# SwiGLU's second projection by Strassen products over all inner columns, and modulation adds on GpSimd

## The chip, the cores and the metric

The kernel runs on 1 core of one Trainium2 chip. The metric is device time in microseconds (us) of one execution. Engines are TensorE (PE, its weight loads PEld), VectorE (DVE), ScalarE (ACT), GpSimd (POOL) and SyncE (SP), which here issues the DMAs, one after the other, in a fixed order. Before the change the time is 2586.88 us, the median of 3 runs (2584.0 to 2587.2).

## The reference

One step of a diffusion model's layer, on 1024 latent and 256 context tokens of width 1024:

```
x += 1/2 * gate1 * SwiGLU_1(adaLN_1(RMSNorm(x)))
h  = adaLN_2(RMSNorm(x)); four head groups A, B, C, D of 256 channels each from h @ w_in
x += gate2 * concat(A, B, C, D) @ w_out
x += 1/2 * gate3 * SwiGLU_2(adaLN_3(RMSNorm(x)))
SwiGLU(h) = (silu(h @ w1a) * (h @ w1b)) @ w2        inner width 2816
adaLN shift/scale/gate from SiLU(c) @ w_mod + b_mod
```

Everything is fp32. The change touches the products with w2, called the down-projections, and the sums that give adaLN's shifts, scales and gates.

## The kernel before

x lies transposed in SBUF: 8 tiles of 128 channels for each of three chunks of tokens, chunk 0 and 1 with 512 latent tokens each, chunk 2 with the 256 context tokens. Every matmul operand is split into a high part, cast by ScalarE, and a low part, subtracted by VectorE, and every product is three matmuls: whi·uh, whi·ul, wlo·uh. The order of the work in time is: norm 1, first up-projection (to 644 us of the span), first down-projection (to 959), the mixer with its four head groups and w_out (to 1700), second up-projection (to 2280), second down-projection (to the end).

An up-projection runs over 22 units, one for each block of 128 inner columns, of 25.06 us each. Its latent part is computed by seven Strassen products already: the 1024 x 256 weights of a block are quartered, their sums (rsum) formed on VectorE from the two loaded halves (raw), and the four quarters of the result put together from p_b and p_t in PSUM; px is the context's. The results, v for the first half of the latent tokens, u for the second and uc for the context, go to DRAM (ud). During the first up-projection the modulation runs as well: GpSimd multiplies a block of w_mod (wh, 256 KB by DMA) with the two conditioning vectors, ScalarE sums each product over its columns (pr, wh into part), and an addition of 2 columns puts it into modT (line 598 of the listing, on VectorE). There are 112 such blocks.

A down-projection (lines 824 to 857) takes two inner blocks at a time, 11 times. It loads two w2 blocks (raw, 512 KB) and the u blocks of them (ur, 256 KB), splits them, multiplies for each chunk c and each of 8 output tiles d the two blocks into one PSUM bank, po, and adds po times the gate into x[c][d], one scalar_tensor_tensor on VectorE. After the last block of chunk c, `done(c)` starts what needs it: in the first down-projection the norm of the chunk (`norm_chunk`: squares on ScalarE, their sums on GpSimd and VectorE, nst over the partitions on TensorE, the root rt, diagonal matrices dg on VectorE, nrs on TensorE, then nt, hh, hl on VectorE, ScalarE and GpSimd) and the copy of x to DRAM (xs); in the second the output's DMAs.

The order of all this on each engine is not that of the source. Every operation is recorded as a node first, and a planner (`Plan`, `issue`) then writes the instructions out in the order that a list schedule with assumed prices gives, nodes of earlier source (with an offset that the code can set) first where they compete. Tiles of one pool and tag are given out in the order of the nodes. Afterwards every engine runs its instructions strictly in that order, and so does SyncE with the DMAs. All operations stand under one line, L394, so that the trace is read by tile names. raw has two buffers, the split weights whi and wlo four each, and po alternates over the PSUM pools PG and PT_.

## Time and profile before

| | |
|---|---|
| median of 3 runs | 2586.88 us (2584.0 to 2587.2) |
| profiled execution, its own time | 2589.14 us |
| its span | 2587.4 us |
| mean granted TensorE clock | 0.982 of 2.4 GHz |
| TensorE busy | 2491.5 us (96%), 14100 matmuls |
| VectorE busy | 1762.7 us (68%) |
| ScalarE busy | 1011.8 us (39%) |
| GpSimd busy | 572.3 us (22%) |
| DMA | 259.42 MB, mean 100 GB/s |

The span runs from the first to the last instruction of the profiled execution; 1.7 us of its time lie around it. Busy shares are averages over stages with different limits, so they are read by stretches in the section on the rows.

### The profile page before, as it was taken

The page shows a single profiled execution, that of the slowest core. Times are in us where ns is not written, and L with a number is a line of the kernel's source. Part 1 is how long each engine was busy: PE and PEld are TensorE (multiplying, and loading weights), DVE is VectorE, ACT ScalarE, POOL GpSimd, SP SyncE. Part 2 cuts the span into 40 slices and gives each one's busy share as a digit, 9 for nine tenths or more (in the row PEclk, how much of TensorE's full clock was granted, in tenths as well). Part 3 has the DMA queues.
Part 4 walks back from the last instruction along what each step waited for, and adds up shares of the span by engine and source line. Part 5 has one row for each costly group of instructions (what it writes and reads, how often), then busy time and mean ns, then how long its engine had stood idle before and what let it go on. Part 6 is the DMA issues. An engine that isn't in the chain of part 4 may idle for free.

```text
span 2587.4 us, 37285 instructions
## 1 busy us (share of the span) xinstructions
PE 2491.5 (96%) x14100; PEld 2096.2 (81%) x14100; DVE 1762.7 (68%) x2819; ACT 1011.8 (39%) x2009; POOL 572.3 (22%) x475
## 2 busy tenths in 40 slices
PE   5899999999999999999999989979999999999999
PEld 3688888888888878888778778868888888888888
DVE  7988888876877674568656575385555555587765
ACT  6555555543212046242476685252222222232110
POOL 1578778830000031122100263130000000000000
PEclk8899999999999999999999999979999999999999
DMA  7143444435422132341301234212122221362312
GB/s 262 60 141 118 146 126 143 124 104 185 150 78 86 49 106 68 103 124 66 109 31 36 81 114 142 98 37 80 54 80 67 66 74 60 97 234 86 94 50 82
DMA packets 146676, 259.42 MB, mean 100 GB/s; under 512 B 15936, under 2 KB 61504, under 8 KB 146496
## 3 DMA queue, kind: packets, MB, share of 16 engines
q1 hardware_dynamic: 146496, 257.04, 31.0%
q8 instruction: 111, 1.82, 0.3%
q14 instruction: 69, 0.57, 0.1%
HBM read 195.11 MB, written 61.87 MB: 99 GB/s over the span
## 4 chain that ended last, share of the span: by engine, by line
PE 74%; DVE 4%; ACT 2%; DMA 1%; issue 1%; POOL 0%; SPq 0%; ACTq 0%
PE po L394 23%; PE p_t L394 12%; PE p_b L394 9%; PE px L394 6%; PE pwo L394 4%; PE fb L394 3%; PE pgd L394 3%; PE ptb L394 2%; PE pyb L394 2%; PE ps L394 2%; PE pd L394 1%; DVE x L394 1%; ACT prob L394 1%; DVE dst L394 1%; PE pgate L394 1%
## 5 line engine op out<-in xcount | busy, mean ns | idle before, releaser
L394 DVE SCALAR_TENSOR_TENSOR x<-po,modT,x 128x512 f32<-128x512 f32 (+1 forms) x528 | 345.3, 661 | 159.7 <-PE po L394 158.4
L394 PE MATMUL po<-uh,whi 128*128 128x512 f32 (+1 forms) x1056 | 377.5, 358 | 5.1 <-DVE x L394 5.1
L394 ACT CAST whi<-raw 128x1024 fp32r<-128x1024 f32 x206 | 213.7, 1048 | 424.7 <-PE px L394 142.2
L394 PE MATMUL po<-uh,wlo 128*128 128x512 f32 (+1 forms) x1056 | 375.3, 355 | 0.0
L394 PE MATMUL po<-ul,whi 128*128 128x512 f32 (+1 forms) x1056 | 373.2, 353 | 0.0
L394 DVE TENSOR_TENSOR wlo<-raw,whi 128x1024 fp32r<-128x1024 f32 x206 | 281.3, 1366 | 100.4 <-ACT whi L394 96.1
L394 PEld LDWEIGHTS po<-uh,whi 128*128 128x128 f32 x1056 | 199.7, 189 | 32.2 <-DVE x L394 5.8
L394 PEld LDWEIGHTS po<-uh,wlo 128*128 128x128 f32 x1056 | 199.3, 189 | 30.9
L394 PEld LDWEIGHTS po<-ul,whi 128*128 128x128 f32 x1056 | 199.5, 189 | 29.5
L394 PE MATMUL px<-hh,whi 128*128 128x256 f32 x704 | 200.2, 285 | 2.3 <-ACT uc L394 1.2
L394 PE MATMUL px<-hl,whi 128*128 128x256 f32 x704 | 200.0, 284 | 0.7 <-DVE hl L394 0.7
L394 PE MATMUL px<-hh,wlo 128*128 128x256 f32 x704 | 198.8, 282 | 0.0
L394 POOL TENSOR_TENSOR pr<-wh,cb 128x512 f32<-128x512 f32 x112 | 172.8, 1543 | 92.3 <-DMA wh<-in_wmodT 60.7
L394 POOL TENSOR_TENSOR wh<-wh,cb 128x512 f32<-128x512 f32 x112 | 186.6, 1666 | 8.8
L394 ACT CAST uh<-ur 128x512 fp32r<-128x512 f32 x110 | 67.3, 622 | 301.7 <-DMA ur<-ud 248.0
L394 POOL TENSOR_TENSOR sq<-sq,sq 128x512 f32<-128x512 f32 (+1 forms) x32 | 37.9, 1185 | 495.3 <-ACT sq L394 492.3
L394 PEld LDWEIGHTS px<-hh,whi 128*128 128x128 f32 x704 | 135.1, 192 | 6.8 <-ACT hh L394 1.6
L394 PEld LDWEIGHTS px<-hl,whi 128*128 128x128 f32 x704 | 134.8, 192 | 5.4 <-DVE hl L394 1.3
L394 PEld LDWEIGHTS px<-hh,wlo 128*128 128x128 f32 x704 | 134.5, 191 | 0.5
L394 ACT ACTIVATE g<-g 128x512 f32<-128x512 f32 x88 | 55.6, 632 | 177.7 <-DVE g L394 177.6
L394 ACT ACTIVATE pr<-pr 128x512 f32<-128x512 f32 x112 | 70.9, 633 | 83.4 <-POOL pr L394 71.4
L394 ACT ACTIVATE wh<-wh 128x512 f32<-128x512 f32 x112 | 70.5, 629 | 56.6 <-POOL wh L394 55.8
(511 smaller groups left out, 6113.3 us busy)
## 6 DMA issues: line engine op xcount, KB each, us to landing
raw<-in_w SPq DMA_DIRECT2D x132, 512.0 KB
wh<-in_wmodT SPq DMA_DIRECT2D x112, 256.0 KB
ur<-ud SPq DMA_DIRECT2D x88, 256.0 KB
ud<-v SPq DMA_DIRECT2D x44, 256.0 KB
ud<-u SPq DMA_DIRECT2D x44, 256.0 KB
x<-in_xT SPq DMA_DIRECT2D x32, 256.0 KB
wmt<-in_wmod SPq DMA_DIRECT2D x32, 256.0 KB
xs<-x SPq DMA_DIRECT2D x32, 256.0 KB
```

Source lines behind the costliest of these rows:

```text
L394: getattr(real, meth)(*[f(v) for v in a], **{q: f(v) for q, v in k.items()})
```

## The change

A down-projection is now nine passes one after the other, each over all inner blocks k and with four PSUM banks. Two passes are the context's: 22 blocks, 256 tokens, the left and the right half of w2's columns. Seven are Strassen products for the latent tokens: inner columns in two halves of 11 blocks, output channels in two halves, tokens in the two chunks. A pass streams its weights, two blocks of 128 x 512 at a time (512 KB), and its u blocks or a sum of them, and at its end adds the four banks into every quarter of x that the product belongs to (1, 1, 1, 4, 1, 2, 2, 3 and 1 quarters). The three sums of w2's quarters and a fourth are formed during the up-projection before it, by `weight_sums` after every second unit: two loads of 512 KB, four half additions on VectorE, three writes to DRAM (sd). The sums of u blocks (t3, t1, t2, t4) are formed on VectorE within the passes. `done` is called for a chunk's half as it is finished; the copies to xs stand ahead of the norm, the tables of the mixer are asked for at its first call, and the first matmuls of the mixer (pa_) take the chunks in the order 2, 1, 0. The modulation's 112 additions go to GpSimd.

```diff
@@ modulation
-        V.tensor_tensor(modT[:, s, f], part, modT[:, s, f] if hf else smv("bmod", 8 * s + f).to_broadcast([P, 2]),
+        G.tensor_tensor(modT[:, s, f], part, modT[:, s, f] if hf else smv("bmod", 8 * s + f).to_broadcast([P, 2]),
                         ALU.add)
@@ buffers
-    BL = 2
+    HF = NFF // 2
     RAW = 2
+    sd = dp.tile([2, 4, HF, P, 512], F32, name="sd")
@@ down
-    def down(n, gate, src, after_block=None, done=None):
...
+    def weight_sums(n, k):
+        lo, hi = slice(0, 512), slice(512, 1024)
+        ra, rb = new_raw(), new_raw()
+        rs = tg.tile([P, 1024], F32, name="rsum", tag="rsum", bufs=1)
+        dma(ra, I["w2"][n, k])
+        dma(rb, I["w2"][n, HF + k])
+        V.tensor_tensor(rs[:, lo], ra[:, hi], rb[:, hi], ALU.add)
+        V.tensor_tensor(rs[:, hi], rs[:, lo], ra[:, lo], ALU.subtract)
+        dma(sd[n, 0:2, k].rearrange("i p n -> p i n"), rs.rearrange("p (i n) -> p i n", i=2))
+        V.tensor_tensor(ra[:, lo], ra[:, hi], ra[:, lo], ALU.subtract)
+        dma(sd[n, 2, k], ra[:, lo])
+        V.tensor_tensor(rb[:, lo], rb[:, lo], rs[:, hi], ALU.subtract)
+        dma(sd[n, 3, k], rb[:, lo])
+
+    def down(n, gate, src, done):
...
+        def t4(k):
+            r = load(HF + k, lo)
+            V.tensor_tensor(r, r, k22[k], ALU.subtract)
+            return r
+        PASSES = [
+            (w2[:, :, lo], None, [(2, 0)]),
+            (w2[:, :, hi], None, [(2, 1)]),
+            (w2[second, :, lo], lambda k: load(HF + k, lo), [c11]),
+            (w2[first, :, lo], lambda k: load(k, lo), [c11, c12, c21, c22]),
+            (sd[n, 3], b22, [c12]),
+            (sd[n, 2], t3, [c21, c22]),
+            (sd[n, 0], t1, [c12, c22]),
+            (sd[n, 1], t2, [c12, c21, c22]),
+            (w2[second, :, hi], t4, [c21]),
+        ]
...
+        for i, (ws, us, outs) in enumerate(PASSES):
+            nk = NFF if us is None else HF
+            w = 256 if us is None else 512
+            ps = [(PT_ if i % 2 else PG)(name="po")[:, :w] for _ in range(4)]
+            for k in range(nk):
+                if k % 2 == 0:
+                    m = min(2, nk - k)
+                    raw = new_raw()
+                    dma(raw[:, :512 * m].rearrange("p (j n) -> p j n", j=m),
+                        ws[k:k + m].rearrange("j p n -> p j n"))
+                    wh, wl = split_w(raw, 512 * m)
...
+                for d in range(4):
+                    q = slice(512 * (k % 2) + d * P, 512 * (k % 2) + (d + 1) * P)
+                    TE.matmul(ps[d], wh[:, q], uh, start=(k == 0), stop=False)
+                    TE.matmul(ps[d], wh[:, q], ul, start=False, stop=False)
+                    TE.matmul(ps[d], wl[:, q], uh, start=False, stop=(k == nk - 1))
...
+            for d in range(4):
+                for c, h in outs:
+                    v = 1 if c == 2 else 0
+                    f = 4 * h + d
+                    V.scalar_tensor_tensor(x[c][f], ps[d], modT[:, gate, f, v:v + 1], x[c][f], ALU.mult, ALU.add)
+            for o in outs:
+                left[o] -= 1
+                if left[o] == 0:
+                    done(*o)
@@ after a unit of the up-projection
+        if nu[0] % 2:
+            plan.offset += 700
+            weight_sums(0, nu[0] // 2)
+            plan.offset -= 700
@@ done1
-        norm_chunk(1, *h2[0], c)
-        for d in range(KT):
+        for d in range(4 * half, 4 * half + 4):
             dma(xs[d][:, t0:t0 + w], x[c][d])
+            tables()
+        if (c, half) in ((2, 1), (1, 1), (0, 1)):
+            norm_chunk(1, *h2[0], c)
@@ mixer's first products
-    for c, (t0, n) in enumerate(CHUNKS):
+    for c in (2, 1, 0):
```

How the planner's order moves is seen at two places. The first is SyncE's queue at the end of the first down-projection; before, the last loads of its weights (raw from w2) are followed by the mixer's and by the copies of x to xs:

```order
L394 DMA raw_7956<-in_w2 128x1024
L394 DMA raw_7970<-in_w2 128x1024
L394 DMA raw_8170<-in_wfm 128x1024
L394 DMA raw_8184<-in_wfm 128x1024
L394 DMA raw_8384<-in_wfm 128x1024
L394 DMA xs_140<-x0_5705 128x512
L394 DMA raw_8398<-in_wfm 128x1024
L394 DMA xs_140<-x0_5746 128x512
```

The changed kernel has there the last four of eight copies of chunk 1, and behind them the last weights (raw_8491) and the first u blocks (ur, from ud) of the last product:

```order
L394 DMA xs_141<-x1_6070 128x512
L394 DMA xs_141<-x1_6084 128x512
L394 DMA xs_141<-x1_6072 128x512
L394 DMA xs_141<-x1_6086 128x512
L394 DMA raw_8491<-in_w2 128x512
L394 DMA ur_8497<-ud_139 128x512
L394 DMA ur_8495<-ud_139 128x512
L394 DMA ur_8501<-ud_139 128x512
L394 DMA ur_8505<-ud_139 128x512
```

Each copy of x waits for the last addition into its tile; the u blocks that the last product subtracts from and multiplies with leave after them. On TensorE of the changed kernel, between the last matmuls of the seventh product (po_8042) and the first of the last one (po_8242, po_8252), stand the norm's matmuls of chunk 1:

```order
L394 MATMUL po_8042<-uh_8344,whi_8322 128x512
L394 MATMUL po_8042<-ul_8347,whi_8322 128x512
L394 MATMUL po_8042<-uh_8344,wlo_8326 128x512
L394 MATMUL nst_8459<-ones_203,sq1_7870 128x1 x4
L394 MATMUL nrs_8467<-dg_800,ones_203 128x128
L394 MATMUL nrs_8467<-dg_808,ones_203 128x128
L394 MATMUL nrs_8467<-dg_7009,ones_203 128x128
L394 MATMUL nrs_8467<-dg_7013,ones_203 128x128
L394 MATMUL po_8242<-uh_8361,whi_8360 128x512
L394 MATMUL po_8252<-uh_8361,whi_8360 128x512
L394 MATMUL po_8242<-ul_8365,whi_8360 128x512
```

Before, matmuls of other output tiles stood around them. The second place is SyncE's queue in a unit of the first up-projection. Before, a unit's two weight loads stand between the modulation's loads (wh) and the unit's results (ud):

```order
L394 DMA wh_2500<-in_wmodT 128x512
L394 DMA raw_2502<-in_w1 128x1024
L394 DMA ud_139<-uc_2033 128x256
L394 DMA wh_2541<-in_wmodT 128x512
L394 DMA wh_2581<-in_wmodT 128x512
L394 DMA wh_2611<-in_wmodT 128x512
L394 DMA wh_2642<-in_wmodT 128x512
L394 DMA wh_2677<-in_wmodT 128x512
L394 DMA ud_139<-v_2243 128x512
L394 DMA raw_2687<-in_w1 128x1024
```

In the changed kernel every second unit has the loads of w2, the writes of their sums (sd) and then the next unit's weights (raw from w1):

```order
L394 DMA raw_2775<-in_w2 128x1024
L394 DMA wh_2784<-in_wmodT 128x512
L394 DMA ud_139<-u_2276 128x512
L394 DMA raw_2831<-in_w2 128x1024
L394 DMA wh_2842<-in_wmodT 128x512
L394 DMA ud_139<-uc_2353 128x256
L394 DMA wh_2875<-in_wmodT 128x512
L394 DMA sd_140<-rsum_2720 128x2x512
L394 DMA sd_140<-raw_2775 128x512
L394 DMA sd_140<-raw_2831 128x512
L394 DMA wh_2928<-in_wmodT 128x512
L394 DMA cb_2941<-in_cb 128x2x512
```

The next rows of that queue are the two loads of w1, raw_2915 and raw_2921, into the same two buffers.

## Rows read from the trace of the kernel before

**Rows 1.** Busy times by stretch: its us; PE, PEld, DVE, ACT, POOL; clock, DMA share, GB/s.

```profile
12.00:110.00 98.00, 73.48 (x462) 50.23 (x463) 86.94 (x161) 57.65 (x103) 28.86 (x20) 0.79 0.43 152
...
493.74:518.80 25.06, 25.06 (x134) 21.42 (x133) 20.71 (x22) 12.90 (x30) 21.27 (x14) 1.00 0.44 131
...
644.00:936.00 292.00, 292.00 (x1510) 249.64 (x1510) 216.06 (x322) 54.45 (x75) 6.72 (x6) 1.00 0.31 96
936.00:976.00 40.00, 33.76 (x175) 28.69 (x174) 35.69 (x58) 26.30 (x44) 21.33 (x18) 0.91 0.25 90
...
952.00:956.00 4.00, 3.75 (x18) 3.46 (x18) 4.00 (x8) 2.14 (x5) 2.44 (x3) 0.50 0.61 214
...
2280.00:2587.00 307.00, 304.02 (x1584) 260.31 (x1583) 220.73 (x331) 45.98 (x63) 0.00 (x0) 1.00 0.29 94
```

**Rows 2.** The chain of waits, its last two pieces on TensorE: start, us, what.

```profile
2277.16 2.83 PE px L394 x24
2279.99 304.05 PE po L394 x1584
```

**Rows 3.** Timeline, TensorE at the seam: start, us, what, [idle before, releaser].

```profile
948.70 0.39 PE L394 MATMUL po<-uh,whi 128*128 128x256 f32 x1 [3.19 <-DVE x L394]
...
955.12 0.41 PE L394 MATMUL po<-uh,wlo 128*128 128x256 f32 x1
...
955.33 0.41 PE L394 MATMUL po<-uh,whi 128*128 128x256 f32 x1
```

**Rows 4.** Groups of VectorE: xcount, busy us, mean ns, idle before.

```profile
L394 DVE SCALAR_TENSOR_TENSOR x<-po,modT,x 128x512 f32<-128x512 f32 x352 | 262.6, 750 | 136.0 <-PE po L394 134.7
...
L394 DVE SCALAR_TENSOR_TENSOR x<-po,modT,x 128x256 f32<-128x256 f32 x176 | 83.8, 483 | 23.7 <-PE po L394 23.7
...
L394 DVE TENSOR_TENSOR modT<-part,small 128x2 f32<-128x2 f32 x56 | 44.7, 799 | 14.5 <-ACT wh L394 14.5
...
L394 DVE TENSOR_TENSOR raw<-raw,rsum 128x512 f32<-128x512 f32 x44 | 40.9, 930 | 0.0
```

**Rows 5.** Timeline at the seam, the norm's work on VectorE and GpSimd.

```profile
938.90 1.95 DVE L394 TENSOR_SCALAR dg<-ident,rt 128x128 f32<-128x128 f32 x4
...
939.49 1.27 POOL L394 TENSOR_TENSOR sq<-sq,sq 128x512 f32<-128x512 f32 x1 [0.98 <-ACT sq L394]
...
941.43 2.06 DVE L394 SCALAR_TENSOR_TENSOR nt<-x,scl,nrs 128x512 f32<-128x512 f32 x3
...
954.55 0.74 POOL L394 TENSOR_TENSOR sq<-sq 128x256 f32<-128x256 f32 x1 [0.72 <-ACT sq L394]
```

**Rows 6.** Timeline: a u block's load issued, and the cast that waits for it.

```profile
681.86 18.35 SPq L394 DMA_DIRECT2D ur<-ud  x6
...
684.56 0.62 ACT L394 CAST uh<-ur 128x512 fp32r<-128x512 f32 x1 [6.22 <-DMA ur<-ud]
```

**Rows 7.** Timeline in the mixer: two weight loads of 512 KB and their splitting.

```profile
1247.97 1.74 SPq L394 DMA_DIRECT2D raw<-in_wc  x2
...
1251.69 1.04 ACT L394 CAST whi<-raw 128x1024 fp32r<-128x1024 f32 x1
...
1253.43 1.22 DVE L394 TENSOR_TENSOR wlo<-raw,whi 128x1024 fp32r<-128x1024 f32 x1
...
1255.00 1.06 ACT L394 CAST whi<-raw 128x1024 fp32r<-128x1024 f32 x1 [2.27 <-DMA raw<-in_wc]
```

**Rows 8.** Timeline in a unit of the first up-projection: its second weight load.

```profile
500.38 0.33 SPq L394 DMA_DIRECT2D raw<-in_w  x1
...
504.26 0.69 DVE L394 TENSOR_TENSOR rsum<-raw 128x512 f32<-128x512 f32 x1 [3.24 <-DMA raw<-in_w]
...
505.69 2.23 DVE L394 TENSOR_TENSOR wlo<-raw,whi 128x1024 fp32r<-128x1024 f32 x1
```

**Rows 9.** Waits of TensorE from 12 to 110: total us, times, longest.

```profile
PE p_t L394 <- DVE t1l L394: 3.0, 2, 2.4
```

More of the change, by code (lines that the diff above doesn't have):

```diff
@@ L944, in write_down, with done1 @@
     h2 = {}
[L946 removed]
+    def done1(c, half):
         t0, w = CHUNKS[c]
+        for d in range(4 * half, 4 * half + 4):
+            dma(xs[d][:, t0:t0 + w], x[c][d])
         if not h2:
             h2[0] = ([None] * 3, [None] * 3)
[L950 to L952 removed]
+            tables()
+        if (c, half) in ((2, 1), (1, 1), (0, 1)):
+            norm_chunk(1, *h2[0], c)
     up(0, ops1, prepare, after_unit)
     assert not mods
[L956 removed]
+    down(0, 2, None, done1)
     hh, hl = h2[0]
```

101 lines of the change are left out of this document (58 added, 43 removed).

## The prediction

> **What bounds the kernel now.** I read the busy times by stretch first [rows 1]. TensorE is busy for all 292.0 us of the first down-projection's stretch, for 304.02 of 307.00 us in the second; it stands only at the start, at the seam between the first down-projection and the mixer (33.76 of 40.00 us) and in the mixer. VectorE has slack everywhere (216.06 of 292.00 us in the first down-projection). Then the chain of waits: the second down-projection is one unbroken piece of 1584 matmuls, 304.05 us, and the up-projection before it ends in px's 24 matmuls of 256 columns in 2.83 us [rows 2]. So a matmul that goes is worth its full time, and only what makes TensorE stand is a cost. At full clock a matmul of 256 columns takes 2.83 / 24 = 0.118 us, one of 512 (304.05 - 528 x 0.118) / 1056 = 0.229; the timeline shows 0.21 for 256 columns [rows 3] in the stretch with granted clock 0.50, which is 1.2 GHz [rows 1].
>
> **What goes.** Per down-projection the latent part falls from 22 inner blocks x 8 x 2 x 3 = 1056 matmuls to 7 products x 11 x 4 x 3 = 924; the context part stays at 528. That is 132 x 0.229 = 30.2 us, for both 60.4 us. VectorE loses the additions into x at every second block: 176 of 0.75 us and 88 of 0.48 per down-projection become 64 wide ones [rows 4]; it was not the bound, so this is worth nothing by itself. The 112 modulation adds (two groups of 56, 0.8 us each, [rows 4]) leave it likewise, beside a full TensorE.
>
> **The seam gains.** Before, TensorE loses 40.00 - 33.76 = 6.2 us there, waiting for the last additions into x between norm work on VectorE (3.19 us the longest, [rows 3]), and then runs some 25 matmuls of 256 columns at 1.2 GHz, which costs 25 x (0.21 - 0.118) = 2.3 us. After the change the context and the second latent chunk are finished before the last product and the mixer's first matmuls take chunks 2, 1, 0: their 4 x 24 x 0.118 + 4 x 24 x 0.229 = 33 us cover the norm of chunk 0. I take all 8.5 us.
>
> **The last product of the first down-projection costs.** On SyncE's queue the loads of its u blocks stand behind eight writes of x1, which wait for the additions of the seventh product. That product writes into three quadrants: 12 additions, about 0.66 us apart (the spacing of three such instructions in a row, [rows 5]), of which the first starts when the first bank is done, 2 us before the product's end; they end at +6. The loads leave at +7.7 and land 2.7 us later (681.86 to 684.56, [rows 6]); then subtract, cast and low part, 0.69 + 0.62 + 0.69 (the steps of 512 columns in [rows 6, 8]): +12.5 at the soonest. But TensorE's order also puts the norm's nst and nrs matmuls of chunk 1 ahead of the product. They wait for ScalarE's squares, GpSimd's sums (1.27 each, [rows 5]), the root and four dg (1.95): about +14.3, and the first ul stands behind the dg on VectorE: +15.5. Then 2.3 us for the low clock (as at the seam) and 2.2 us more for the second or third block, whose subtraction and ul stand behind a dozen norm instructions. In all 20 us; at least 11 (the loads alone with a quicker queue), at most 28 if the norm is served whole before the second block. In the second down-projection there is no norm and these loads are prepared two products earlier: 0.
>
> **The context products cost.** They come first, with 256 columns: one 512 KB load of weights serves only 24 x 0.118 = 2.83 us of TensorE. There are two load buffers, and each is held from the issue over landing, cast and low part. The mixer shows that round: issues at 1247.97 and a little over a microsecond later, casts at 1251.69 and 1255.00 (the second waited for its DMA), 1.05 for the cast, 1.22 for the low part [rows 7]. That is 3.7 to 5.6 + 1.05 + 1.22 = 6.0 to 7.9 us a buffer, 3.0 to 3.9 us a load of two: 0.2 to 1.1 us late each, against a lead of some four loads prepared during the up-projection (11 us, used once). For 22 loads that is between 22 x 0.17 - 11, which is below 0, and 22 x 1.1 - 11 = 13; the seam between the two products adds 1.9 (one addition of 0.48 and one low part of 1.22 at its end). Taken: 3.6 + 1.9 = 5.5 us per down-projection, 11 for both, a little above the middle of the two ends, since the slow one of the two loads shared its time with other transfers, as these do with the u blocks; 0 to 15 each.
>
> **The fourth pass costs** 1 us each, 2 together: its 16 additions take 16 x 0.66 = 10.6 to 16 x 0.75 = 12 us, and the four u blocks prepared ahead give 4 x 12 x 0.229 = 11.
>
> **The weight sums cost** in the up-projections. In every second unit two more 512 KB loads, four half sums and three writes go through the same two load buffers, ahead of the next unit's own weights. Before, in the unit from 493.74 the second load is issued at 500.38, summed from 504.26 and its low part done by 508 [rows 8]; the next unit starts at 518.80, so some 11 us are spare. The extra round takes a landing of 3.9 [rows 8], four sums of up to 0.93 [rows 4] and a write that has to land before the buffer is loaded again (2.7 for the nearest row, [rows 6]): 3.9 + 3.7 + 2.7 = 10.3. So under 1 us remains. Nothing is late on paper, some of 22 units will be: 4 us at the first unit, where the four sums come ahead of an addition that TensorE waits for (it waits there for VectorE already, 3.0 us, [rows 9]), and 7 for all others, between 0 and 30.
>
> **The tail**: the last addition is 512 wide, 0.75 for 0.48 [rows 4]: +0.3.
>
> **Sum**: 60.4 + 8.5 - 20 - 11 - 2 - 4 - 7 - 0.3 = 24.6 us less. The profiled execution took 2589.1 (its span 2587.4 and 1.7 around it), 2.3 above the median of the runs shown: 2589.1 - 24.6 - 2.3 = 2562.2.
>
> **The rivals.**
> *Nearly the whole gain.* The context loads land as fast as the quickest row (0 there), the units keep their microsecond (0), the last product starts at +11, first unit 1, fourth pass 1: 68.9 - 13.3 = 55.6, which gives 2531. For it: the load share is only 0.29 to 0.31 in the down-projections [rows 1]: there is room for faster transfers. Against: the order on SyncE's queue is fixed, and a wait there is not made up.
> *Low clock in the context products, slower.* If every late load lets TensorE fall to 1.2 GHz, 24 matmuls cost 24 x (0.21 - 0.118) = 2.2 us more; half of 44 loads, with the wait itself still there, is 49 + 11 = 60 us in place of 11, so 2562 + 49 = 2611. It decides from 14 loads on (2.2 x 14 = 31 on top of what I count: 6 us above before). For it: in the first stretch, where TensorE is busy for 73.48 of 98.00 us, its granted clock is 0.79, and at the seam one stand of 3.19 us took it to 0.50 [rows 1, 3]. Against: that stand was three times the longest counted here; and at the low clock 24 matmuls take 5.0 us, longer than a load, so that the stand, and with it the cause, goes.
> The Trainium skill (TensorE: Matmul & The Clock Gate, HAM oscillation — how this bites in real kernels) describes this case: when the matmuls on one tile of weights are shorter than the wait for the next, each tile starts at the slow clock, again and again. The stretch with clock 0.50 behind a stand of 3.19 us agrees with it as far as it goes; no row of this kernel shows it repeated. By that page all 44 loads would be hit, 44 x 2.2 = 97 us more, so 2659.
> *GpSimd becomes the pace of the first up-projection.* It is busy 21.27 of 25.06 us of a unit [rows 1]. Five adds on two columns come to it; the nearest row is 0.74 for 256 columns [rows 5], and each waits for ScalarE's sum: five times 0.6 plus five waits of 0.5 make 26.8, 1.7 us over, in some 20 units 34 us. The loads of modulation weights then hold SyncE's queue and the unit's weights behind them. In place of my 7 that gives 2589, no difference. Against: the adds are placed one or two multiplications later than the sums they read, so most waits are short.
> *That the change doesn't do what it says* I exclude: the instruction counts of the changed program are those above.
>
> **How the numbers follow.** The forecast has 0.52 with a range of its own from 2546 to 2580; the whole gain 0.17; the low clock 0.10; GpSimd's pace 0.15; 0.06 for several of these together, above 2600. A measurement of this kernel tells 0.2% (5.2 us) from no change. Faster: all of the first two, a small part of the third rival: 0.70. Same: half of GpSimd's case and a little of the forecast's upper end: 0.12. Slower: low clock, the rest of GpSimd's, the rest: 0.18. Range 2532 to 2598.
>
> **What would show it.** In the profile after: 1452 po matmuls per down-projection; a stand of TensorE of some 15 us and a lower clock just ahead of the last 132 of the first; short waits of po for wlo, behind the loads, in the first 62 us of each down-projection, with the clock at 1.00; a seam to the mixer without stand; waits of p_t, p_b and px for whi or wlo below 1 us per unit. I am wrong if TensorE stands under 11 us there, if the context products take over 80 us, or if units of the first up-projection take over 25.6 us on the mean.

## The result and the profile after

The changed kernel takes 2643.3 us, the median of 4 runs (2640.34 to 2649.2), against 2587.04 (2584.0 to 2588.02, 4 runs) before: ratio 1.0222, 95% interval 1.0203 to 1.0242. It is slower by some 56 us, where 24.6 less had been forecast. The profiled execution took 2649.2 us, its span is 2647.4, 60.0 longer than before. The busy times by stretch are read first, as in [rows 1]: us, then PE, PEld, DVE, ACT, POOL, granted clock, DMA share, GB/s.

```profile
110.00:560.00 450.00, 420.98 (x2125) 352.74 (x2124) 337.13 (x329) 237.25 (x539) 355.36 (x309) 0.97 0.50 160
560.00:682.00 122.00, 120.60 (x641) 103.01 (x640) 80.04 (x107) 41.80 (x63) 9.20 (x9) 1.00 0.49 163
682.00:965.00 283.00, 260.67 (x1345) 219.49 (x1345) 185.35 (x253) 111.57 (x159) 16.98 (x14) 0.96 0.58 190
965.00:1003.00 38.00, 34.98 (x132) 26.61 (x130) 31.26 (x37) 19.73 (x31) 10.38 (x7) 0.89 0.22 68
1003.00:1069.00 66.00, 60.22 (x304) 51.22 (x305) 29.79 (x55) 28.55 (x50) 9.05 (x6) 0.95 0.25 79
...
2344.00:2387.00 43.00, 35.40 (x268) 33.56 (x268) 16.46 (x21) 11.99 (x14) 0.00 (x0) 0.92 0.87 310
2387.00:2428.00 41.00, 35.08 (x270) 32.42 (x270) 19.03 (x23) 12.14 (x12) 0.00 (x0) 1.00 0.81 263
2428.00:2643.00 215.00, 215.00 (x923) 173.12 (x922) 151.57 (x210) 79.78 (x113) 0.00 (x0) 1.00 0.44 142
```

TensorE now has holes in the first up-projection (420.98 of 450.00), in the first down-projection (260.67 of 283.00) and in the two context products of the second (43.00 and 41.00 us, some 35 busy). The second down-projection was one unbroken piece before [rows 2]; in the same 450 us of the first up-projection TensorE was busy for 440.56 us:

```profile
110.00:560.00 450.00, 440.56 (x2303) 374.85 (x2302) 380.16 (x431) 253.38 (x577) 346.47 (x216) 0.99 0.43 132
```

Cut at the first and last matmul of each part, the stretches of the two profiled executions are, in us:

| | first up | first down | to the mixer (pa_) | mixer | w_out | second up | second down | tail |
|---|---|---|---|---|---|---|---|---|
| before | 643.9 | 315.7 | 58.3 | 580.7 | 101.8 | 579.2 | 303.9 | 3.6 |
| after | 681.8 | 320.8 | 65.9 | 592.1 | 101.6 | 581.9 | 298.5 | 4.3 |

Of the 37.8 us in the first up-projection 4.3 lie in its first unit and 33.5 in units 1 to 17 (440.4 before, 474.0 after). In units 18 to 21, where no modulation is left, it is 100.2 in both, though sums of weights are formed there as well. So the sums alone are not it. The loss lies in the unit behind each round of sums: units 1, 3, 5 to 17 take 29.8 us on the mean, the units between them 25.7.

How far one execution can be trusted is seen where kernels share a first half. Six of them run the changed first half in the same order of instructions on every engine (the changed kernel, e3, e4, e5, e6, e11): their units 1 to 17 take 474.0, 466.3, 471.1, 472.5, 468.7 and 467.9 us, and their first up-projections end between 673.6 and 682.0. Three run that of the kernel before (before, e7, e8): 440.4, 434.8 and 437.8 us, the ends between 639.7 and 644.1. So between single executions of this stretch a difference of less than some 8 us says nothing.

### The profile page after: what moved, and what is told of

It is laid out like the page before. It is cut to its first block, busy times and chain, and to the rows that moved or that the text cites. A ratio compares the mean times of both kernels' runs of the same rounds, so it can differ in the third digit from the quotient of the medians.

```text
span 2647.4 us, 37054 instructions
## 1 busy us (share of the span) xinstructions
PE 2486.1 (94%) x13836; PEld 2072.4 (78%) x13836; DVE 1718.8 (65%) x2633; ACT 1127.8 (43%) x2162; POOL 607.5 (23%) x587
## 4 chain that ended last, share of the span: by engine, by line
PE 64%; DMA 5%; DVE 5%; ACT 2%; issue 1%; POOL 1%; SPq 0%; POOLq 0%; ACTq 0%; DVEq 0%
PE po L394 17%; PE p_t L394 11%; PE p_b L394 8%; PE px L394 5%; PE pwo L394 4%; PE fb L394 3%; PE pgd L394 3%; DMA raw<-in_w 3%; PE ptb L394 3%; PE pyb L394 2%; PE ps L394 2%; DVE wlo L394 1%; PE pd L394 1%; ACT whi L394 1%; DVE x L394 1%
## 5 line engine op out<-in xcount | busy, mean ns | idle before, releaser
L394 DVE TENSOR_TENSOR wlo<-raw,whi 128x1024 fp32r<-128x1024 f32 (+1 forms) x290 | 366.1, 1263 | 319.0 <-ACT whi L394 295.9
L394 ACT CAST whi<-raw 128x1024 fp32r<-128x1024 f32 (+1 forms) x290 | 296.3, 1026 | 484.0 <-DMA raw<-in_w 132.8
L394 PE MATMUL po<-uh,whi 128*128 128x512 f32 x616 | 244.2, 399 | 2.7 <-ACT uh L394 2.7
L394 PE MATMUL po<-ul,whi 128*128 128x512 f32 x616 | 245.4, 398 | 0.4 <-DVE ul L394 0.4
L394 PE MATMUL po<-uh,wlo 128*128 128x512 f32 x616 | 244.5, 398 | 0.2 <-DVE wlo L394 0.2
L394 ACT ACTIVATE g<-g 128x512 f32<-128x512 f32 x88 | 55.3, 628 | 237.5 <-DVE g L394 237.5
L394 PEld LDWEIGHTS po<-uh,whi 128*128 128x128 f32 x616 | 116.5, 190 | 31.1 <-ACT uh L394 3.1
L394 PEld LDWEIGHTS po<-ul,whi 128*128 128x128 f32 x616 | 116.8, 190 | 29.5 <-DVE ul L394 1.5
L394 PEld LDWEIGHTS po<-uh,wlo 128*128 128x128 f32 x616 | 116.6, 189 | 28.8 <-DVE wlo L394 0.9
L394 PE MATMUL po<-uch,whi 128*128 128x256 f32 x352 | 99.1, 292 | 15.4 <-ACT whi L394 15.3
L394 DVE TENSOR_TENSOR ul<-ur,uh 128x512 fp32r<-128x512 f32 x132 | 91.8, 712 | 28.9 <-ACT uh L394 21.5
```

The source lines that it names most:

```text
L394: getattr(real, meth)(*[f(v) for v in a], **{q: f(v) for q, v in k.items()})
```

## Experiments

Times beside an experiment's are those of the kernel before on the same chip. Where no interval is given, the version ran once. The stretches are those of the profiled execution.

**1 and 2. The two edits of the up-projection apart.**

```diff
@@ e1: the changed kernel, adds back on VectorE
-        G.tensor_tensor(modT[:, s, f], part, ...
+        V.tensor_tensor(modT[:, s, f], part, ...
@@ e2: the kernel before, adds on GpSimd
-        V.tensor_tensor(modT[:, s, f], part, ...
+        G.tensor_tensor(modT[:, s, f], part, ...
```

> The changed kernel with the 112 modulation adds back on VectorE, all else as changed. The changed kernel's first up-projection ends at 681.7 us, before's at 644.0; units 1 to 17 lose 33.5 us in all. Theory A (GpSimd's in-order adds set the pace): the units come back to 25.06 us as before, the up-projection ends near 650. Theory B (the weight sums' extra round through the two load buffers is the late one, GpSimd only beside it): it ends within 8 us of 681, since VectorE gets 0.8 us per add on top, perhaps later.

> The kernel before with only the 112 modulation adds moved to GpSimd; no weight sums, no Strassen products in the down-projection. Theory A: the first up-projection ends near 675 instead of 644, the total near 2620. Theory B: it ends within 3 us of 644, the total within 6 us of 2587. If both are needed together, this one and the one with the adds on VectorE both stay near 644 to 655.

e1 takes 2626.06 us (before 2584.1), e2 2594.37. Units 1 to 17 make a square: 440.4 without either edit, 440.1 with the adds alone, 452.5 with the weight sums alone, 474.0 with both. The adds cost there only where the sums are formed too. Their price is smaller than this square has it: in e1 a part of the modulation is left for units 18 and 19, and units 18 to 21 take 104.5 us instead of 100.2. By the ends of the whole up-projection (662.7 in e1, 663.9 in e10, which has the same first half, and 673.6 to 682.0 with the adds on GpSimd) it is 10 to 19 us.

**3 and 4. The context products.**

```diff
@@ e3: a third load buffer from the second up-projection on
-    RAW = 2
+    RAW = 3
@@ e4: in the second down-projection the context's passes last
+        if n:
+            PASSES = PASSES[2:] + PASSES[:2]
```

> The changed kernel with three load buffers instead of two from the second up-projection on. The second down-projection's two context products take 42.8 and 40.2 us, 31.4 each at full rate. If the two buffers' round bounds them (issue to landing 4 to 4.5, cast 1.05, low part 1.23: 3.4 us a load): both fall to 32 to 35 us, 14 to 18 us less in all. If the DMA engines bound them, whose packets carry the prefetched u blocks too (share 0.8 there): they stay above 38 each. The second up-projection stays at 25.06 us a unit.

> The changed kernel with the two context products of the second down-projection after the seven others instead of ahead of them. If the u blocks fetched ahead for later products share the DMA engines with the weights and so make the loads late: the context products, now with nothing fetched beside them, take 32 to 35 us each (31.4 at full rate) instead of 42.8 and 40.2. If the two load buffers' round alone bounds them, they stay near 38 each (3.4 us a load). The first product of the seven may wait some us at the start for its u blocks.

e3 takes 2622.87 us, and its second down-projection 285.6 for 298.5. (Of the 26.3 us between the two profiled executions another 8.4 lie in the first up-projection, which e3 does not touch.) Its two context products, by stretch:

```profile
2331.00:2370.00 39.00, 34.06 (x267) 33.04 (x267) 15.87 (x18) 12.01 (x13) 0.00 (x0) 0.96 0.94 334
2370.00:2401.00 31.00, 31.00 (x266) 31.00 (x265) 17.43 (x21) 12.04 (x13) 0.00 (x0) 1.00 0.96 333
```

334 GB/s are moved, and the second is unbroken; the first still takes 39.0 us. With two buffers, each is held too long; in the changed kernel's timeline this is one round of one buffer (start, us, what, [idle before, releaser]):

```profile
753.70 0.38 SPq L394 DMA_DIRECT2D raw<-in_w  x1
754.13 1.88 SPq L394 DMA_DIRECT2D ur<-ud  x4
757.71 3.24 SPq L394 DMA_DIRECT2D raw<-in_w  x2
758.23 1.05 ACT L394 CAST whi<-raw 128x1024 fp32r<-128x1024 f32 x1 [1.81 <-DMA raw<-in_w]
759.31 1.23 DVE L394 TENSOR_TENSOR wlo<-raw,whi 128x1024 fp32r<-128x1024 f32 x1 [1.63 <-ACT whi L394]
```

From the issue at 753.70 to the end of the low part at 760.54 are 6.8 us, 3.4 a load with two buffers, against 2.83 that TensorE takes for one; four u blocks are issued in the same round. In e4, where no u blocks are loaded ahead beside them, the first context product falls to 31.1 us and the second to some 35, but the product that now comes first waits for its u blocks (46.6 us for 30.8), and the whole gains nothing: 2645.91.

**5. The place of the moving operand.**

```diff
-                    uh, ul = TG(F32R, "uh"), TG(F32R, "ul")
+                    uh, ul = (HG if n else TG)(F32R, "uh"), (HG if n else TG)(F32R, "ul")
```

> The changed kernel with the split u operands of the second down-projection's seven products (uh, ul, the moving side of the matmuls) in the pool HG, which lies at 20 to 102 KB of a partition, instead of TG, at 116 to 177 KB. In the changed kernel its 512-column matmuls come every 0.2333 us, before's, whose u lay in HG, every 0.229; in both kernels p_t of t2, t3, t4 (TG) comes at 0.233 and p_b and p_t of t1 (HG) at 0.229. If the place of the moving operand sets it: each product's 132 matmuls take 30.2 us instead of 30.8. If it is the order (three matmuls a bank instead of six): they stay at 30.8. The first down-projection's stay at 30.8 either way.

2632.18 us (before 2583.63). The last piece of the chain of waits, after and in e5:

```profile
2425.53 217.96 PE po L394 x940
```
```profile
2414.64 211.79 PE po L394 x924
```

924 matmuls of 512 columns take 211.79 us in e5, 0.229 each. After, 940 of which 16 have 256 columns take 217.96: less 16 x 0.118 that is 0.234. The granted clock is 1.00 in both. In these seven products only the pool that holds uh and ul differs. The same 4 to 5 ns show in the up-projections of both kernels between operands in the one and in the other pool. Whether the place of the pool in the memory counts or something else about it was not tested.

e5 has a second effect, which was not expected: its context products take 73.9 us together, for 83.0 in the changed kernel, with two load buffers in both. With uh and ul in HG the planner lays fewer loads of u blocks beside them: 8 for 21 in the first 40 us of the second down-projection. So the 11 us that e5 gains are not the price of the pool alone, and this shows more plainly than e4 that the u blocks loaded ahead make the context's weights late. In e7 below, with HG and the third buffer, both context products run without a hole.

**6. The norm of chunk 1 behind the last product** of the first down-projection.

```diff
-        if (c, half) in ((2, 1), (1, 1), (0, 1)):
+        if (c, half) == (2, 1):
             norm_chunk(1, *h2[0], c)
+        if (c, half) == (0, 1):
+            norm_chunk(1, *h2[0], 1)
+            norm_chunk(1, *h2[0], 0)
```

> The changed kernel with the norm of chunk 1 in the first down-projection called after the last product instead of after the seventh, so that the last product's u blocks are given their tiles first. If the norm ahead of it makes the last product late (17.9 us of standing and 7.6 more within it): it starts within 8 us of the seventh's end and takes 30.8 to 33. The seam to the mixer then has the norms of chunks 1 and 0 behind it and its pa_ products, 65.9 us in the changed kernel, get longer by 5 to 15; the net gain is 10 to 20 us. If SyncE's copies of x1 alone hold the u loads: the standing stays over 10 us.

2617.35 us: 26 less than the changed kernel's median. The first down-projection falls from 320.8 to 296.6, its last product from 38.4 to 30.8 with no stand ahead of it; the seam to the mixer grows from 65.9 to 74.6, and the first up-projection was 6.6 shorter in this run. What stands ahead of that product in the changed kernel:

```profile
946.11 7.99 DVE L394 SCALAR_TENSOR_TENSOR x<-po,modT,x 128x512 f32<-128x512 f32 x12
...
946.88 7.56 SPq L394 DMA_DIRECT2D xs<-x  x8
...
956.35 5.47 SPq L394 DMA_DIRECT2D ur<-ud  x11
...
959.50 1.87 PE L394 MATMUL nst<-ones,sq 128*128 128x1 f32 x8 [12.62 <-DVE sq L394]
959.74 0.69 DVE L394 TENSOR_TENSOR ur<-ur 128x512 f32<-128x512 f32 x1 [0.30 <-DMA ur<-ud]
...
962.71 2.08 PE L394 MATMUL nrs<-dg,ones 128*128 128x128 f32 x8 [1.34 <-DVE dg L394]
963.16 1.28 DVE L394 TENSOR_TENSOR ul<-ur,uh 128x512 fp32r<-128x512 f32 x2
964.37 0.55 PEld L394 LDWEIGHTS po<-uh,whi 128*128 128x128 f32 x2
964.44 1.20 PE L394 MATMUL po<-uh,whi 128*128 128x512 f32 x2
```

The additions end at 954.1, the u blocks leave at 956.35, nst runs at 959.50, and po resumes at 964.4, 17.7 us after the end of the seventh product. In e6 both are gone, the norm ahead of the product and the loads behind the copies: the last product's u blocks are issued before the eight copies.

**7 and 8. The second half alone.** Modulation, first up- and first down-projection are those of the kernel before (`down_blocks`, the old `down`); in the second half stand the nine passes and the weight sums, with three load buffers and uh, ul in HG.

```diff
@@ e7, against the kernel before
-    RAW = 2
+    RAW = 3
-    down(1, 8, xs, done=done2)
+    down(1, 8, xs, done2)
...
+                    uh, ul = HG(F32R, "uh"), HG(F32R, "ul")
@@ e8, against e7: the latent x is loaded at the second pass
-                    for c in range(3):
-                        load_x(c, src)
+                    load_x(2, src)
+                if i == 1 and k == 0:
+                    load_x(0, src)
+                    load_x(1, src)
```

> A version that keeps the first down-projection, its up-projection and the modulation adds of before, and takes the Strassen products, weight sums, three load buffers and u operands in HG for the second down-projection alone. From the parts: second down-projection 285.6 with three buffers less 7 x 0.6 = 281.4, against before's 303.9; second up-projection within 2 us of before's 579.2; tail +0.7; the clock in the mixer may go either way by some us at shifted times, but nothing is shifted ahead of it here. So 20 to 23 us faster than before, near 2565.

> The same with x for the two latent chunks loaded (4 MB) at the start of the second context product instead of the first. If those loads beside the first context product hold its weights back (it took 38.9 us with three buffers, the second 31.1): it falls to 32 to 34 us, 5 us less in all than the version before, near 2560. If not, or if the loads then hold up the second context product: no difference.

e7: 2559.67 us (2555.84 to 2564.92), before 2583.63, ratio 0.9906 (0.9888 to 0.9923). e8: 2558.07, 0.989 (0.9871 to 0.9908), no difference from e7. The last piece of e7's chain of waits answers to [rows 2]:

```profile
2278.81 273.71 PE po L394 x1452
```

It is unbroken, 30.3 us shorter than the 304.05 before: the forecast's 30.2 for one down-projection, in full. By the medians the whole kernel gains 24.0 us, with a spread of 9 us over its four executions; where the other 6 are was not looked into.

**9 and 12. GpSimd's waits.** After, GpSimd waits for ScalarE's sum in front of half of its adds; this is what the rival on GpSimd's pace had priced. Total us, times and longest between 110 and 560 us, after:

```profile
POOL modT L394 <- ACT wh L394: 50.0, 54, 3.0
POOL pr L394 <- DMA wh<-in_wmodT: 19.6, 21, 2.1
POOL pr L394 <- ACT pr L394: 15.6, 10, 3.5
```

```diff
-        part = cbp.tile([P, 2], F32, name="part", tag="part", bufs=2)
+        part = cbp.tile([P, 2], F32, name="part", tag="part", bufs=6)
...
+        pend.append((hf, s, f, part))
+        if len(pend) > 2:
+            mod_add()
@@ e12 only: ordered behind the newest multiplication
+        plan.after = last[0]
```

> The changed kernel with the adds still on GpSimd, but each recorded two blocks of modulation weights later (part gets six buffers), so that the sum it reads on ScalarE is older. In the changed kernel GpSimd waits 50 us in 54 waits for ScalarE in front of these adds (110 to 560 us), and units 1 to 17 take 474.0 us; with the adds on VectorE 452.5, without weight sums 440. If that waiting is what the adds cost: units 1 to 17 take 450 to 458. If it is the adds' own time on GpSimd, or another order of loads on SyncE's queue: they stay over 465.

> The changed kernel with every modulation add held behind the multiplications two blocks later on GpSimd (in the order of the program too), so that it never reads a sum still being made. If the waits of these adds for ScalarE (50 us in 54 waits) are what they cost: GpSimd's waits in front of them fall under 10 us, the mean round of the two load buffers from 18.9 to about 18, units 1 to 17 from 474 to 450 to 458. If not, the waits go and units 1 to 17 stay over 465.

In e9 the planner put the adds back where they had been (46.9 us in 54 waits; 2641.47 us), so it says nothing. In e12 the waits of the adds are gone:

```profile
POOL pr L394 <- DMA wh<-in_wmodT: 35.4, 37, 3.0
POOL pr L394 <- ACT pr L394: 21.2, 13, 3.6
POOL pr L394 <- ACT cb L394: 6.8, 1, 6.8
```

Still it takes 2643.71 us, and units 1 to 17 473.2. So the waits are not the cause, and my theory up to here fell. GpSimd's pace as such was not changed by it: the other waits grew, its busy time in these 450 us is 373.93 us for 355.36, and it gets through 104 blocks for 102.

**13. Two of the four half sums left out.**

```diff
-        V.tensor_tensor(ra[:, lo], ra[:, hi], ra[:, lo], ALU.subtract)
+        if n:
+            V.tensor_tensor(ra[:, lo], ra[:, hi], ra[:, lo], ALU.subtract)
```
(and the same for rb)

> The changed kernel in which two of the four sums of each pair of w2 blocks are not formed during the first up-projection (the loaded halves are written to DRAM as they are), so that its first down-projection computes with other numbers. Adds stay on GpSimd; loads and writes stay. If the round of the two buffers sets the pace: it loses two VectorE instructions of 0.9 to 1.8 us in one of three rounds, some 3 us per two units, so units 1 to 17 fall by 8 times 3 = 24 us, to about 450. If GpSimd's adds set it alone: they stay over 468.

2639.24 us; units 1 to 17 take 464.8 for 474.0, with all the loads and writes of the sums in place. The fall of 24 us that was expected did not come, and 464.8 is within 2 us of what the unchanged first half takes in e3 (466.3). So e13 shows no effect of two sums less.

**14 and 15. GpSimd's multiplications made short.** The timeline of the changed kernel shows what VectorE and GpSimd do to each other (VectorE, then GpSimd):

```profile
482.76 1.83 DVE L394 TENSOR_TENSOR rsum<-raw 128x512 f32<-128x512 f32 x1 [3.66 <-DMA raw<-in_w]
484.63 1.67 DVE L394 TENSOR_TENSOR rsum<-rsum,raw 128x512 f32<-128x512 f32 x1
486.33 1.82 DVE L394 TENSOR_TENSOR raw<-raw 128x512 f32<-128x512 f32 x1
488.07 0.68 DVE L394 TENSOR_TENSOR raw<-raw,rsum 128x512 f32<-128x512 f32 x1
...
482.75 1.29 POOL L394 TENSOR_TENSOR wh<-wh,cb 128x512 f32<-128x512 f32 x1
484.00 1.75 POOL L394 TENSOR_TENSOR pr<-wh,cb 128x512 f32<-128x512 f32 x1
485.71 0.64 POOL L394 TENSOR_TENSOR modT<-part,modT 128x2 f32<-128x2 f32 x1
486.31 1.29 POOL L394 TENSOR_TENSOR wh<-wh,cb 128x512 f32<-128x512 f32 x1
```

They take turns. VectorE's first sum starts with GpSimd's multiplication and ends 0.55 after it, 1.83 us for 0.68; the next multiplication, 1.75 for 1.29, ends 1.16 after that sum; the add of two columns, 0.64, ends when the second sum has ended. Only the last sum finds GpSimd standing, and takes 0.68.

In e14 GpSimd multiplies 8 of 512 columns, in e15 256, and ScalarE's first sum takes the other columns from the loaded block, so that the modulation is not the reference's.

```diff
-        G.tensor_tensor(pr, w, cbs[0][:, 0], ALU.mult)
-        S.activation(pr, pr, AF.Identity, accum_out=part[:, 0:1])
-        G.tensor_tensor(w, w, cbs[0][:, 1], ALU.mult)
+        G.tensor_tensor(pr[:, :8], w[:, :8], cbs[0][:, 0, :8], ALU.mult)
+        S.activation(pr[:, 8:], w[:, 8:], AF.Identity, accum_out=part[:, 0:1])
+        G.tensor_tensor(w[:, :8], w[:, :8], cbs[0][:, 1, :8], ALU.mult)
@@ e15: 256 for 8
```

> The changed kernel with GpSimd's multiplications of the modulation made short: 8 of the 512 columns in each of the two; ScalarE sums the other 504 of one of them from the loaded block itself (so the second projection's modulation is not the reference's). Loads, their order on SyncE's queue and the five adds on GpSimd stay. In the changed kernel VectorE's four half sums of weights take 1378, 1634, 1401 and 840 ns between 110 and 560 us, and 680 to 692 where GpSimd stands still; the low parts 1546 and 1749 for 1222. Theory (VectorE is held up by GpSimd's multiplications whenever both read the on-chip memory): the sums take 0.69 and the low parts 1.22, a round of the load buffers 18.9 - some 1 to 1.5, and units 1 to 17 of the first up-projection fall from 474.0 to 445-457 us. Rival (the third round of loads and writes through the two buffers makes it, whatever VectorE does): the sums get shorter but units 1 to 17 stay above 466.

> The same with 256 of the 512 columns in GpSimd's multiplications (ScalarE sums 256 instead of 512; the modulation is not the reference's). Theory (VectorE held up by GpSimd): half the overlap, sums of 1.0 us, units 1 to 17 between the two, 455-467. Rival (the round of loads): as the changed kernel within 4 us, 470-478.

2592.22 and 2601.55 us (before 2582.96). Units 1 to 17 take 432.4 and 429.5 us, less than before the change, with all loads, writes and sums in place: more than the theory had expected, since TensorE now has no wait there worth naming (in e14 it is busy for 450.00 of the 450 us). The two edits take away more than the collisions, though. GpSimd's own work is cut (95.43 and 232.70 us busy for 355.36), ScalarE's first sum no longer reads GpSimd's product, and the planner laid SyncE's queue anew, with mostly 7 to 10 blocks of modulation weights in a unit for 5 to 7, so that the modulation ends two to four units earlier. The same VectorE groups after and in e14, between 110 and 560 us (count | busy us, mean ns | idle before); the rows of raw and rsum hold the up-projection's own sums and those of w2 alike:

```profile
L394 DVE TENSOR_TENSOR wlo<-raw,whi 128x1024 fp32r<-128x1024 f32 x48 | 74.2, 1546 | 55.2 <-ACT whi L394 44.0 <-PE p_t L394 11.1
L394 DVE TENSOR_TENSOR raw<-raw 128x512 f32<-128x512 f32 x23 | 37.6, 1634 | 0.6
L394 DVE TENSOR_TENSOR u<-p_t,u 128x512 f32<-128x512 f32 x51 | 34.6, 679 | 0.8 <-PE p_t L394 0.8
L394 DVE TENSOR_TENSOR rsum<-rsum,raw 128x512 f32<-128x512 f32 x24 | 33.6, 1401 | 0.3
L394 DVE TENSOR_TENSOR rsum<-raw 128x512 f32<-128x512 f32 x24 | 33.1, 1378 | 23.9 <-DMA raw<-in_w 23.9
```
```profile
L394 DVE TENSOR_TENSOR wlo<-raw,whi 128x1024 fp32r<-128x1024 f32 x55 | 67.2, 1222 | 37.1 <-ACT whi L394 37.1
...
L394 DVE TENSOR_TENSOR raw<-raw 128x512 f32<-128x512 f32 x27 | 18.7, 691 | 0.7
...
L394 DVE TENSOR_TENSOR rsum<-rsum,raw 128x512 f32<-128x512 f32 x27 | 18.6, 690 | 0.3
...
L394 DVE TENSOR_TENSOR rsum<-raw 128x512 f32<-128x512 f32 x27 | 18.5, 684 | 2.1 <-DMA raw<-in_w 2.0
```

A sum takes 0.69 us without the multiplications, 1.4 to 1.6 beside them. u<-p_t,u, which has one operand in PSUM, keeps its 679 ns beside them.

**10 and 11. Both halves mended; the order of the mixer's first products.**

```diff
@@ e10: the edits of e1, e6, e5 in both halves, and RAW = 3 in the second half
@@ e11: the changed kernel
-    for c in (2, 1, 0):
-        t0, n = CHUNKS[c]
+    for c, (t0, n) in enumerate(CHUNKS):
```

> The changed kernel with all that the runs so far point to, in both halves: adds on VectorE, u operands of the seven products in HG, norm of chunk 1 behind the last product, three load buffers from the second up-projection on; the first half keeps its weight sums and two load buffers. From the parts: first up-projection 662, first down-projection 296.6 less 7 x 0.6 = 292, pa_ 75, mixer 585, w_out 102, second up-projection 579, second down-projection 273.5, tail 4: 2572 of span. If the first half's products pay after all it is under the 2559.7 of the version with the second half alone; I expect 2566 to 2580, slower than that one and faster than before.

> The changed kernel with the mixer's first products in before's order of chunks (0, 1, 2) instead of 2, 1, 0. With 2, 1, 0 TensorE waits 5.1 us for ScalarE's copies of the context's results, which stand behind the norm of chunk 0, and the 288 matmuls take 65.9 us, in before 58.3. If that order is what used up the seam's gain: 58 to 62 us here. If chunk 0's norm is late for any order: TensorE now waits for hh of chunk 0 directly, 10 to 15 us between the last product and the third chunk's matmuls, and from the last product to the end of pa_ it takes as long or longer.

e10 takes 2569.8 us (5 runs; before 2585.54), ratio 0.994 (0.992 to 0.996): faster than before, slower than e7, since units 1 to 17 still take 454.9. e11 takes 2644.3, no better than the changed kernel: with chunk 0 first the products run in 58.1 us instead of 65.9, but TensorE waits longer for the norm ahead of them: from the last po to the last pa_ it takes 71.4 us for 66.3.

**16 to 18. All computed, one of GpSimd's two multiplications on VectorE.**

```diff
-        G.tensor_tensor(w, w, cbs[0][:, 1], ALU.mult)
+        V.tensor_tensor(w, w, cbs[0][:, 1], ALU.mult)
@@ e16: in e10    e17: in e10, the adds on GpSimd    e18: in e7
```

> Both halves mended (adds on VectorE, parts of u blocks in the lower part of the memory, norm of chunk 1 behind the last product, three load buffers in the second half), and in the modulation the second of the two multiplications of a block (wh by cb) on VectorE instead of GpSimd; nothing is left out. Without this last edit: units 1 to 17 of the first up-projection 454.9 us, time 2569.8. Theory (VectorE and GpSimd hold each other up, so that less work on GpSimd counts more than 112 times 0.69 us more on VectorE): units 1 to 17 take 430 to 442, time 2545 to 2558. Rival (VectorE has no room for 112 more multiplications): 450 or more, time 2565 or more.

> The same with the modulation's adds on GpSimd, as in the changed kernel; nothing is left out. Theory: with GpSimd's multiplications halved the adds there cost nothing or less than 5 us: units 1 to 17 at 428 to 442, time 2543 to 2558. Rival (the adds on GpSimd cost 20 us whenever the weight sums are formed): 450 or more, 2565 or more.

> The kernel with the change in the second half alone (time 2559.67; first up-projection as before, units 1 to 17 at 434.8 there), and the second multiplication of the modulation on VectorE; nothing is left out. Theory: the collisions of the kernel before go too: units 1 to 17 at 426 to 432, time 2552 to 2558. Rival: the additional work on VectorE delays the units, 440 or more, 2565 or more.

Medians of 4 runs, before 2584.73 (7 runs): e16 2557.0, ratio 0.9889 (0.987 to 0.9908); **e17 2540.21**, 0.983 (0.9813 to 0.9846); e18 2550.96, 0.9868 (0.9853 to 0.9883). Units 1 to 17 take 442.4, 429.4 and 428.1 us. In e16 VectorE has 97 multiplications more in this stretch than in e10 (the second row), and its busy time is 377.92 us for 372.32; TensorE's is 440.01 for 430.85:

```profile
110.00:560.00 450.00, 440.01 (x2287) 373.26 (x2287) 377.92 (x539) 232.17 (x525) 144.05 (x95) 0.99 0.49 162
```
```profile
110.00:560.00 450.00, 430.85 (x2226) 361.88 (x2225) 372.32 (x436) 235.42 (x531) 305.42 (x198) 0.99 0.48 161
```

In e16 GpSimd has only the other multiplication, and stands for two thirds of the stretch:

```profile
L394 POOL TENSOR_TENSOR pr<-wh,cb 128x512 f32<-128x512 f32 x95 | 144.1, 1516 | 311.1 <-DMA wh<-in_wmodT 245.2 <-ACT pr L394 33.8 <-ACT wh L394 17.8
```

So what e16 still loses against 426.0 us is not GpSimd's pace; 13 of these 16 us go when VectorE is rid of the adds. e17 against e16 shows that the adds are better on GpSimd, once that has room: the edit of the change which looked guilty in the square of e1 and e2 gains 13 us of units 1 to 17 here. e17 is the fastest version, 1.7% below before.

## Why the prediction was wrong

The terms as forecast, and the difference of the two profiled executions:

| term | forecast | measured |
|---|---|---|
| matmuls that go | -60.4 | -60.4, but +8.0 for uh, ul in TG |
| seam | -8.5 | -4.1 |
| last product of the first down | +20 | +25.3 |
| context products, both | +11 | +35.4 |
| pass behind them, fourth pass | +2 | +2.2 |
| weight sums, both up-projections | +11 | +40.5 |
| tail | +0.3 | +0.7 |
| mixer and w_out | 0 | +11.2 |

The right column makes +58.8 of the 60.0 us. Two of the signs that the prediction set itself came: the second pair of context products takes 83 us, over 80, and units 1 to 17 take 27.9 us on the mean, over 25.6.

**The weight sums** are the step that failed first. It counted a round of 10.3 us against 11 that were spare, with the sums at 0.93, the mean of [rows 4]. That mean mixes the first up-projection with the second, where GpSimd does little: 4 x 0.93 became 5.3 beside it, and every low part in the same round got longer too (1546 ns for 1222). In the changed kernel a round, from the second load of w2 to the second load of the next weights, takes 12.9 us on the mean of the eight that lie beside the modulation (4.2 to the first sum, 5.2 for the four sums, 3.5 to the next load), and 10.3 in the two behind it, where the sums take 2.7: there the forecast's 10.3 holds. The two loads of w2 also leave 5.4 us apart, since loads of modulation weights that wait for their buffers stand between them; the forecast counted from the second. More work of a kind that collides was added to the stretch in which GpSimd works; the 2.23 us for a low part in [rows 8], against 1.22 in [rows 7], had shown the collision before the change. The third rival, GpSimd as the pace of the first up-projection, had the right place and about the right size (34 us; units 1 to 17 give 33.5 here, and 26 to 34 over the executions of the changed first half). Its account of the waits for ScalarE's sums is refuted by e12, which took them away without effect. Cutting GpSimd's multiplications takes the whole loss away (e14, e15, and e17 with everything computed): so it is the weight sums and GpSimd's multiplications together that cost.

By which way is open in part. Longer sums and low parts on VectorE are one way, as the turns show; GpSimd's own pace on SyncE's queue is the other, and e14, e15 and e17 shorten both. In the changed kernel, between 110 and 560 us, SyncE stands 232.4 us for buffers of modulation weights:

```profile
SPq L394 <- ACT wh L394: 232.4, 80, 7.8
```

That standing alone costs nothing either (300.5 us in e2, 221.5 in e17), and a round as long as 12.4 us costs next to nothing in e17. Only in e16 is one of the two shown by itself: with GpSimd idle for 311 us, VectorE's own load costs 13 us. That the adds cost 10 to 19 us with the sums and nothing without fits the turns in the timeline, where an add stands in line with VectorE's sums; how much of it is the adds' own turns was not separated.

The Trainium skill (SBUF — State Buffer, SBUF: two separate sides) describes the turns: VectorE and GpSimd share a pair of ports, held by one of them for a whole instruction, and a VectorE operation with two inputs in SBUF needs it. The trace agrees with both halves of it: the turns at 482.76, and 679 ns for u<-p_t,u whatever GpSimd does. The prediction weighed GpSimd's time and VectorE's time each by itself, and did not weigh that rule.

**The context products** were right in mechanism and too small: +15.1 and +20.3 us, on or over the upper end of 0 to 15 each. The forecast round of 6.0 to 7.9 us holds (6.8). At 3.4 a load 22 loads are 22 x 0.57 = 12.5 us late, with the 1.9 of the seam 14.4: so the first loss is the forecast's own sum without the 11 us that it took off for a lead of four loads. That lead did not show. e3 shows that the two buffers are it, e4 and e5 that the u blocks loaded ahead share in it, and e7 that with both mended nothing is left.

**The last product** was right as told: 17.7 + 7.6 = 25.3 us within the bounds of 11 to 28, by the queue and the norm as described. e6 takes both away at once, and the stand with them; it does not tell them apart. It also shows that the stand pays for cover at the seam: there 24 us are saved and 9 come back.

**The seam** came about half. Before, 11.7 us were lost in the down-projection's end and 3.0 in pa_ (58.3 less 55.3 for its matmuls at full clock); after, 10.6 in pa_, of which 5.1 is one wait for a copy (xa) that stands behind chunk 0's norm on ScalarE.

**The fourth pass** cost nothing: its 31.0 us are those of the passes behind it, and the 2.2 us in the table lie in the pass right behind the context products.

**The moving operand** was not in the sum at all: the change put uh and ul into another pool, which cost 8.0 us in both down-projections (924 x 2 x 4.3 ns). e5 shows it.

**The mixer** was not in the sum either. Its matmuls stand in the same order, and yet it takes 592.1 us for 580.7. The same piece of it, before and after:

```profile
1449.00:1469.00 20.00, 16.05 (x143) 12.17 (x142) 15.63 (x26) 14.97 (x42) 8.92 (x10) 1.00 0.53 160
```
```profile
1505.00:1528.00 23.00, 18.77 (x143) 14.43 (x142) 15.97 (x26) 14.58 (x40) 8.90 (x10) 0.82 0.44 133
```

The same 143 matmuls, VectorE as busy as before, and a granted clock of 0.82, a mean of 2.4 and 1.2 GHz, for 1.00, which is 2.4 GHz throughout. Such a difference also arises without any change. The mixer of the kernel before, with the same instructions on each engine, takes 581 us in the profiled execution, 584 to 585 in e7 and 586 in e2, which reaches it only 0.3 us later; that of the changed kernel takes 592, 587 to 588 in e1, e3, e4 and e5, 586 in e12 and 583 in e6. So the two ranges overlap, most of the 11 us can be such a spread, and the moment at which the mixer starts does not explain it. What sets the clock at a given moment of the mixer stays open.

**The rivals.** The low clock in the context products came in small part: the granted clock is 0.95 and 0.96 in the first two (36 and 42 us) and 0.92 and 1.00 in the second two, which is at most 7 us of the 35 (1 less the clock, times the stretch); the rest of the price is in the waits. The rule that the prediction quotes beside this rival speaks of matmuls shorter than the wait for the next weights; 2.83 us of matmuls against forecast waits of 0.2 to 1.1 is not that case, so its 2659 did not follow from the rule. The whole gain is real in the second half (e7, 30.3 of 30.2).

## What to carry to other kernels

Price a VectorE instruction from the stretch where it will run, not from a mean over the program: if its two operands lie in SBUF and GpSimd works beside it, it can take twice as long, and moving work from GpSimd to VectorE can make the kernel faster. Where a change turns long products into short ones per load, compare the round of one load buffer (issue, landing, cast, low part), divided by the number of buffers, with TensorE's time for one load. When an edit has two halves, time each alone and both together before either is blamed; here the adds looked guilty beside a crowded GpSimd and were a gain once it had room. Before a difference between single executions is given a cause, see how far the same instructions spread from one execution to the next: here 8 us in one stretch and 9 in another.

## What the runs showed of the hardware that was not expected

- A GpSimd add of two columns takes 0.20 us with VectorE out of the way (at 496.36 in the changed kernel) and 0.64 in turn with a sum (at 485.71).
- Halving GpSimd's multiplications (e15) did as much for units 1 to 17 as all but removing them (e14): 429.5 and 432.4 us, of 426.0 that 17 units of 25.06 take. The whole up-projection ends at 636.5 and 627.5 us; the difference lies in the first unit.
- A matmul of 512 columns takes 0.229 or 0.233 us at the same granted clock, by the pool that its moving operand lies in.
- The same instructions run at other granted clocks from one execution to the next: 581 to 586 us for the mixer of the kernel before, 583 to 592 for that of the changed one.
